# A two-layer streaming encoder: the four mixers run in 14 steps laid a projection apart, the row constants get a buffer of their own, and more of the conditioning is computed beside the mixers

## The chip, the cores and the metric

The kernel runs on one core of a Trainium2 chip. The metric is the device time of one execution in microseconds, from the first to the last instruction and what lies around them. Of three runs of the kernel before, the median was 1093.91 us (1090.06 to 1305.59). The rows below come from a further, profiled execution, which took 1088.88 us. The numbers are float32; a difference of about 2% is what a comparison of this kernel can tell from no change.

## The reference

One sequence of 256 tokens of width 1024 passes two layers. Each layer is a half-step SwiGLU FFN (width 2816), a token mixer, and a second half-step FFN; each is fed by an RMSNorm whose shift, scale and gate come from a vector c.

```python
for l in range(DEPTH):
    cond = (c_act @ ada_w[l] + ada_b[l])[:, None, :]
    sh1, sc1, g1, sh2, sc2, g2, sh3, sc3, g3 = jnp.split(cond, N_MOD, axis=-1)
    h = modulate(rmsnorm(x, norm_g[l, 0]), sh1, sc1)
    x = x + 0.5 * g1 * swiglu(h, ffn1_w13[l], ffn1_w2[l])
    h = modulate(rmsnorm(x, norm_g[l, 1]), sh2, sc2)
    x = x + g2 * hybrid_mixer(h, ...)
    h = modulate(rmsnorm(x, norm_g[l, 2]), sh3, sc3)
    x = x + 0.5 * g3 * swiglu(h, ffn2_w13[l], ffn2_w2[l])
return rmsnorm(x, final_g)
```

The mixer projects h to 3600 columns and splits them into four parts of width 256: forgetting attention (fox), mLSTM, retention with rotary (ret) and Mamba-2 SSD (ssd). Each makes a decayed score matrix per head, multiplies it with its values, and gates the result; the four results go through one output projection.

## The kernel before

Activations are kept feature-major (128 features by 256 tokens, eight tiles). Each float32 product is three matmuls on rounded parts: a weight tile `raw` of 128x1024 is loaded by a DMA on SP's queue, ScalarE (ACT) rounds it into `whi` (L199), VectorE (DVE) subtracts to get the rest `wlo` (L200), and TensorE (PE) adds `whi` by the high part of the input, `whi` by the low part and `wlo` by the high part (`mm3`, L215 to L219). So every 512 KB of weights cost DVE one *split* and PE 24 matmuls of about 256 columns. Four raw buffers and four pairs of split buffers let the loads and splits run ahead.

The conditioning matrix is 144 blocks of 128x1024. All but a few of the very first section are summed on DVE: a DMA loads a block into `araw`, and one DVE instruction (L258, here a *background sum*) multiplies it by c and adds up. The table `BG` says after how many projection or weight steps of a stage how many such blocks are put in; `flush` puts in what is missing before a stage needs it.

A stage starts with a normalisation: the sums of squares are reduced by two matmuls (`stat`, L346), ACT and POOL take the inverse root (`rs`, L367, L368), two matmuls spread it (L373) and ACT copies it to the row `R` (L377). The first two projections of a stage run on the unnormalised x (`uh`, `ul`), and their results are multiplied by R afterwards. All later ones need the normalised input: for each of eight tiles DVE makes `xr` (L402), ACT the high part `hh` (L406), DVE the low part `hl` (L407).

The mixers (`mixers_in`) are a list, `ORDER`: `p.rq` is the projection for `rq`, other names are steps that take a projection's result and run one part of a mixer. 14 projections of two weight tiles each run in the order of the list. `rotary` turns rq and rk (a 512-column matmul, then four DVE instructions), `gates` is a chain of some 20 small DVE instructions, `conv_silu` a convolution on DVE (L607), `ssd_front`, `ret_front`, `mlstm_front`, `fox_front` make score matrices (tiles `pp`, in PSUM banks `pb`), and `pv_tm` (L722) multiplies them with the values. In this list each mixer's scores and its product with the values are one step.

The order of instructions on an engine is set by a list scheduler in the framework: it keeps to the program's priorities (the order of the code, unless `tc.high_priority` raises a part) and to its own estimate of when inputs are ready. On the chip each engine runs its list strictly in order, and so does SP's DMA queue.

`row` (L628) holds 792 constants, sent to all 128 partitions by one DMA (L629) as the mixers begin; its tile takes memory that the FFN before it used. ACT reads it first in L821.

Of the kernel before, what the change touches and what calls it, by code (L numbers as in the profile page):

```python
# [15 lines left out]
P = 128  # L16
D = 1024
T = 256
# [22 lines left out]
WO_GROUPS = ((0, 1), (3, 2))  # L41

WO_TURNS = 2, 5
# [6 lines left out]
BG = [((16, 15), (5, 13), (6, 12)), ((8, 0), (5, 8)), ((14, 14), (6, 0), (10, 18)), ((14, 14), (6, 0), (10, 18)),  # L50
      ((8, 0), (5, 8)), ((14, 8),)]
R0 = 6
NW = 11, 0, 2, 6
HP, HP2 = 30, 100
ORDER = """p.rq p.rk rq h p.mv gates rk p.sx mv sx p.sbc sbc p.rv p.mq p.mk rows rv ssd p.fk mk mq mlstm p.fq
 ret fq p.fv fk fv p.sz sz fox p.mo foxb mo p.rg ssdb rg""".split()
# [5 lines left out]
def trunk_kernel(  # L62
# [119 lines left out]

    cond = [cp.tile([P, 72], F32, name=f"cond{l}") for l in range(L)]
# [137 lines left out]
    def stat_begin():  # L321
        s = Stat()
        s.R = s.rows = None
        s.ps = ps_c.tile([P, 2], F32, tag="c", name="stat")
        s.acc = tp.tile([P, T], F32, tag="acc", name="acc")
        s.sq = {}
        return s
# [43 lines left out]
    def stat_R(v, o, pin=False):  # L371
        for t in range(2):
            m = pe.matmul(o[:, t * P:(t + 1) * P], lhsT=v[:, t:t + 1].to_broadcast([P, P]), rhs=ident, start=True, stop=True)  # L373
            if pin:
                tc.keep_in_program_order(m)
        R = tp.tile([P, T], F32, tag="R", name="R")
        act.activation(out=R, in_=o[:, :T], func=AF.Copy)  # L377
        return R
# [138 lines left out]
    def ffn_in(fp, l, i, w13, w2, st, done):  # L517
# [47 lines left out]
        for c in range(NS if first else ND, NFF):  # L565
            if first and c == NS + 3:
                load_more()
            w = wload(w13(l, c), 2, KT, P)
            o = bank_a().rearrange("p (a b) -> p a b", a=2)
            mm_fm(o[:, 1, :], w[0], h)  # L570
            mm_fm(o[:, 0, :], w[1], h)
            gate_out(c, o[:, 0, :], o[:, 1, :])
            background()
# [42 lines left out]
    def mixers(l, st, done):  # L616
        with tc.tile_pool(name=f"mp{l}", bufs=1) as mp:
            bg_pool[:] = mp, 1
            spare[:] = None, 0
            return mixers_in(mp, l, st, done)  # L620

    def mixers_in(mp, l, st, done):
# [5 lines left out]
        row = mp.tile([P, NC_ROW], F32, name="row")  # L628
        sp.dma_start(out=row, in_=row_in[l].partition_broadcast(P))  # L629
# [222 lines left out]
        def ssd_front(sx, sc, la, dt):  # L852
# [54 lines left out]
        def ssd_back(xd, z2):  # L907
# [11 lines left out]
            turns.append((3, y))  # L919

        def mlstm_front(mlf, arow, mq, mv):
# [41 lines left out]
            num = pv_tm(*transpose_p(p0, p1), mv)  # L963
            return num, head_norm(num, "m", den)

        def fox_front(arow, fq):
# [23 lines left out]
            return p0, p1, den  # L990

        def fox_back(p0, p1, den, fv):
            num = pv_tm(*transpose_p(p0, p1), fv)
# [3 lines left out]
            put_y(0, to_fm(y))  # L997
# [12 lines left out]
        def ret_front(rq, rv):  # L1010
# [11 lines left out]
            dve.tensor_tensor(out=p1, in0=o.rearrange("p (h t) -> p h t", h=4), in1=dec[:, :, :P], op=ALU.mult)  # L1022
            num = pv_tm(p0, p1, rv)
# [24 lines left out]

        def e_rq():
            v["rq"] = mp.tile([P, 2, T], F32, tag="q", name="rq", bufs=2)  # L1050
            rotary(rotated("rq"), lambda r, rs: dve.tensor_tensor(out=v["rq"], in0=r, in1=rs, op=ALU.add))
# [27 lines left out]
        def e_ssd():  # L1079
            v["xd"] = ssd_front(v["sx"], v["sc"], v["la"], v["dt"])  # L1080
# [14 lines left out]
        def e_ret():  # L1095
            scaled(*ret_front(v["rq"], v["rv"]), "rl")

        def e_mlstm():
            scaled(*mlstm_front(v["gl"][:, :, 4:8], v["arow"], v["mq"], v["mv"]), "ml")
# [8 lines left out]
        def e_fox():  # L1108
            v["fp"] = fox_front(v["arow"], v["fq"])

        def e_foxb():
            fox_back(*v["fp"], v["fv"])
# [7 lines left out]
        def e_mo():  # L1120
# [8 lines left out]
            put_y(1, to_fm(y))  # L1129

        def e_rg():
# [4 lines left out]
            turns.append((2, y))  # L1136

        parts = dict(rq=e_rq, rk=e_rk, sx=e_sx, sbc=e_sbc, mv=lambda: e_v("mv"), rv=lambda: e_v("rv"), fv=lambda: e_v("fv"),
                     gates=e_gates, rows=e_rows, ssd=e_ssd, mq=e_mq, mk=e_mk, ret=e_ret, mlstm=e_mlstm, fq=e_fq, fk=e_fk,
                     fox=e_fox, foxb=e_foxb, sz=e_sz, ssdb=e_ssdb, mo=e_mo, rg=e_rg, h=lambda: h.extend(norm_h(st)))  # L1140
        for x in ORDER:
            if x.startswith("p."):
                project(x[2:])
            else:
                parts[x]()
# [6 lines left out]
        for g, grp in enumerate(WO_GROUPS):  # L1152
            for n, k in enumerate(WO_TILES):
# [172 lines left out]
```

## Time and profile before

| | |
|---|---|
| profiled execution | 1088.88 us, span 1087.1 us |
| runs, median (lowest to highest) | 1093.91 us (1090.06 to 1305.59) |
| PE busy | 1065.9 us, 98% of the span |
| PE weight loads busy | 1049.6 us, 97% |
| DVE busy | 853.6 us, 79% |
| ACT busy | 536.7 us, 49% |
| POOL busy | 69.8 us, 6% |
| granted TensorE clock | full speed in every slice |

The page gives, for the slowest (here the only) core, the busy time of each engine over the span, the costliest groups of instructions with the idle time just before them, and who ended that idle time. "A <- B: x" means that A sat idle for x us until B's result came. Two consecutive matmuls overlap in the records, so a record of 0.28 us starts 0.12 us after the one before it. The stages lie, in us from the span's start: FFN 0 to 199, mixers of layer 0 from 199 (their first normalisation ends at 220) to 350, FFN to 549, FFN of layer 1 to 727, mixers of layer 1 to 880, FFN to the end.

### The profile page before, as it was taken

The numbers are of one execution on the slowest core, as the hardware profiler recorded it, in microseconds if no ns is written. First come the engines' busy times: TensorE is split into PE (matmuls) and PEld (weight loads), VectorE is DVE, ScalarE is ACT, GpSimd is POOL, SyncE is SP. The second block draws the span as 40 slices with busy tenths as digits, with TensorE's granted clock in tenths as the row PEclk, the third lists the DMA queues.
The fourth block names the chain that finished last, engine by engine and source line by source line (L and its number), as shares of the span: only waits on it lengthen the run. The fifth ranks groups of instructions, "written<-read, shape, count | busy, mean of one in ns | idle before, by whom it ended". The sixth has DMA issues, their size and how long they took to land.

```text
span 1087.1 us, 21715 instructions
## 1 busy us (share of the span) xinstructions
PE 1065.9 (98%) x8745; PEld 1049.6 (97%) x8745; DVE 853.6 (79%) x1495; ACT 536.7 (49%) x893; POOL 69.8 (6%) x86
## 2 busy tenths in 40 slices
PE   8999999989999999999999999999999999999998
PEld 6999999989999999999999999999999999999998
DVE  6899889789957989888589888767987688876551
ACT  4555444355545745443474543355535566454441
POOL 0000001200012200000100000012001130000010
PEclk9999999999999999999999999999999999999999
DMA  9889989947424589888568988765644465865531
GB/s 367 333 299 347 324 323 329 304 160 244 143 97 154 187 293 343 296 294 284 187 213 280 333 302 303 265 203 192 222 147 142 131 214 195 290 225 183 184 126 40
DMA packets 73879, 258.17 MB, mean 237 GB/s; under 512 B 10161, under 2 KB 12465, under 8 KB 73266
## 3 DMA queue, kind: packets, MB, share of 16 engines
q1 hardware_dynamic: 73490, 256.26, 68.5%
q8 instruction: 69, 1.13, 0.4%
q10 hardware_dynamic: 288, 0.52, 0.1%
q14 instruction: 32, 0.26, 0.1%
HBM read 255.70 MB, written 1.05 MB: 236 GB/s over the span
## 4 chain that ended last, share of the span: by engine, by line
PE 78%; DMA 8%; DVE 8%; ACT 3%; issue 2%; POOL 1%; SPq 0%; ACTq 0%; DVEq 0%; POOLq 0%
PE pa L217 22%; PE pa L219 22%; PE pa L218 22%; DMA raw<-in_w2a_dram 3%; DMA araw<-in_ada_dram 3%; DVE wlo L200 2%; PE pa L678 2%; PE pa L676 2%; PE pa L677 1%; ACT whi L199 1%; DVE araw L258 1%; PE pb L729 1%; DVE ul L395 1%; ACT pp L987 1%; DMA row<-in_row_dram 1%
## 5 line engine op out<-in xcount | busy, mean ns | idle before, releaser
L199 ACT ACTIVATE whi<-raw 128x1024 fp32r<-128x1024 f32 (+1 forms) x340 | 354.1, 1046 | 287.7 <-PE pa L218 81.1
L200 DVE TENSOR_TENSOR wlo<-raw,whi 128x1024 fp32r<-128x1024 f32 (+1 forms) x340 | 409.1, 1211 | 87.8 <-ACT whi L199 87.1
L217 PE MATMUL pa<-hh,whi 128*128 128x256 f32 x1424 | 403.8, 284 | 1.5 <-ACT whi L199 0.8
L218 PE MATMUL pa<-hl,whi 128*128 128x256 f32 x1424 | 404.1, 284 | 0.0
L219 PE MATMUL pa<-hh,wlo 128*128 128x256 f32 x1424 | 403.0, 283 | 0.5 <-DVE wlo L200 0.5
L217 PEld LDWEIGHTS pa<-hh,whi 128*128 128x128 f32 x1424 | 273.2, 192 | 3.4 <-ACT whi L199 2.1
L219 PEld LDWEIGHTS pa<-hh,wlo 128*128 128x128 f32 x1424 | 273.2, 192 | 1.2 <-DVE wlo L200 0.7
L218 PEld LDWEIGHTS pa<-hl,whi 128*128 128x128 f32 x1424 | 273.3, 192 | 0.5 <-issue 0.5
L217 PE MATMUL pa<-sh,whi 128*128 128x256 f32 x704 | 199.2, 283 | 0.0
L218 PE MATMUL pa<-sl,whi 128*128 128x256 f32 x704 | 199.2, 283 | 0.0
L219 PE MATMUL pa<-sh,wlo 128*128 128x256 f32 x704 | 199.2, 283 | 0.0
L258 DVE CUSTOM_DVE_ANT_0 araw<-araw,cact 128x1024 f32<-128x1024 f32 x128 | 157.4, 1230 | 44.7 <-DMA araw<-in_ada_dram 44.2
L217 PEld LDWEIGHTS pa<-sh,whi 128*128 128x128 f32 x704 | 135.2, 192 | 0.0
L218 PEld LDWEIGHTS pa<-sl,whi 128*128 128x128 f32 x704 | 135.2, 192 | 0.0
L219 PEld LDWEIGHTS pa<-sh,wlo 128*128 128x128 f32 x704 | 135.2, 192 | 0.0
L534 ACT ACTIVATE sh<-s 128x256 fp32r<-128x256 f32 x88 | 36.1, 411 | 109.8 <-DVE s L527 104.7
L338 POOL TENSOR_TENSOR acc<-acc,sq 128x256 f32<-128x256 f32 x40 | 36.2, 906 | 697.8 <-ACT sq L333 696.8
L218 PE MATMUL pa<-ul,whi 128*128 128x258 f32 x208 | 59.1, 284 | 2.3 <-DVE ul L395 2.3
L217 PE MATMUL pa<-uh,whi 128*128 128x258 f32 x208 | 59.7, 287 | 0.0
L676 PE MATMUL pa<-whi,hh 128*128 128x256 f32 (+1 forms) x192 | 56.4, 294 | 3.1 <-ACT hh L406 3.1
L219 PE MATMUL pa<-uh,wlo 128*128 128x258 f32 x208 | 58.8, 283 | 0.0
L678 PE MATMUL pa<-whi,hl 128*128 128x256 f32 (+1 forms) x192 | 55.4, 292 | 0.0
(262 smaller groups left out, 1313.8 us busy)
## 6 DMA issues: line engine op xcount, KB each, us to landing
araw<-in_ada_dram SPq DMA_DIRECT2D x128, 512.0 KB, 5.6
raw<-in_w13b_dram SPq DMA_DIRECT2D x88, 512.0 KB, 5.0
raw<-in_w13a_dram SPq DMA_DIRECT2D x76, 512.0 KB, 5.9
raw<-in_w2a_dram SPq DMA_DIRECT2D x44, 512.0 KB, 5.5
raw<-in_w2b_dram SPq DMA_DIRECT2D x44, 512.0 KB, 4.6
raw<-in_wfm_dram SPq DMA_DIRECT2D x32, 512.0 KB, 4.9
raw<-in_wtm_dram SPq DMA_DIRECT2D x24, 512.0 KB, 4.4
raw<-in_wo_dram SPq DMA_DIRECT2D x16, 512.0 KB, 4.8
```

What stands on the lines that cost most here:

```text
L199: act.activation(out=hi, in_=raw, func=AF.Copy)
L200: dve.tensor_tensor(out=lo, in0=raw, in1=hi.bitcast(F32), op=ALU.subtract)
L217: pe.matmul(o, lhsT=wh, rhs=xh, start=first, stop=False, **kw)
L218: pe.matmul(o, lhsT=wh, rhs=xl, start=False, stop=False, **kw)
L219: pe.matmul(o, lhsT=wl, rhs=xh, start=False, stop=last, **kw)
L258: dve.tensor_tensor_reduce(out=raw, in0=raw, in1=cact, scale=0.5, scalar=0.0, op0=ALU.mult, op1=ALU.add, accum_out=cond[l][:, i:i + 1])
L338: eng.tensor_tensor(out=s.acc, in0=s.acc, in1=sq, op=ALU.add)
L395: dve.scalar_tensor_tensor(out=s.ul[:, k, :T], in0=xT[:, k, :], scalar=s.G[:, k:k + 1], in1=s.uh[:, k, :T].bitcast(F32), op0=ALU.mult, op1 ...
L534: act.activation(out=sh[:, c, :], in_=s, func=AF.Copy)
L676: pe.matmul(os[t], lhsT=h[0][:, k, ts], rhs=wh[:, y, :], start=(k == 0), stop=False)
L677: pe.matmul(os[t], lhsT=h[0][:, k, ts], rhs=wl[:, y, :], start=False, stop=False)
L678: pe.matmul(os[t], lhsT=h[1][:, k, ts], rhs=wh[:, y, :], start=False, stop=(k == KT - 1))
```

## The change

Five edits, of one piece each:

1. `ORDER` is rewritten. ssd, ret, mlstm and fox become generators that stop (`yield`) after their scores and, for mlstm and fox, before and after the transposes; each stop is one entry of the list, with at least one projection between. `rqe` takes rq's raw result out of PSUM, and `rq` (the rotary part) follows a projection later. ret runs before mlstm and within ssd; the gates sz and rg come before fox.
2. `row` becomes a buffer of its own (`rows_of`), loaded in the first FFN of each layer (`i == 0 and c == NS + 4`). To make room, `acc` and `R` have one buffer instead of two.
3. The normalisation `h` of the mixers is put at raised priority.
4. `BG` changes: 12 instead of 8 background sums are planned in the mixers of layer 0 and 14 instead of 8 in those of layer 1, spread over nearly all projections, with two `araw` buffers (`MB = 2`) instead of one; fewer in the second FFNs.
5. The output projection takes ssd and ret first, then fox and mlstm; the last fox step and two transposes lie between its first tiles (`WO_STEPS`).

The number of instructions of each kind is the same on every engine (8489 on PE, 1497 on DVE, 877 on ACT); only their order and buffers differ.

```diff
-WO_GROUPS = ((0, 1), (3, 2))
-WO_TURNS = 2, 5
+WO_GROUPS = ((3, 2), (0, 1))
-BG = [((16, 15), (5, 13), (6, 12)), ((8, 0), (5, 8)), ((14, 14), (6, 0), (10, 18)), ((14, 14), (6, 0), (10, 18)),
-      ((8, 0), (5, 8)), ((14, 8),)]
+BG = [((16, 17), (9, 21)), ((2, 0), (12, 12)), ((15, 16), (5, 0), (8, 12)), ((15, 16), (5, 0), (8, 12)),
+      ((14, 14),), ((14, 8),)]
+MB = 2
-ORDER = """p.rq p.rk rq h p.mv gates rk p.sx mv sx p.sbc sbc p.rv p.mq p.mk rows rv ssd p.fk mk mq mlstm p.fq
- ret fq p.fv fk fv p.sz sz fox p.mo foxb mo p.rg ssdb rg""".split()
+ORDER = """p.rq p.rk rqe h p.mv rq gates rk p.sx mv sx p.sbc sbc p.rv rows rv p.mq ssd ret p.mk ssd mq ret
+ p.sz ssd mk mlstm p.rg sz mlstm ssdb p.fk rg mlstm p.fq fk mlstm p.fv fq fox p.mo fv fox mo""".split()
+WO_STEPS = {1: "fox", 4: "turn", 6: "turn"}
...
-        s.acc = tp.tile([P, T], F32, tag="acc", name="acc")
+        s.acc = tp.tile([P, T], F32, tag="acc", name="acc", bufs=1)
...
+            if i == 0 and c == NS + 4:
+                rows_of[l] = cp.tile([P, NC_ROW], F32, tag="row", name="row", bufs=1)
+                sp.dma_start(out=rows_of[l], in_=row_in[l].partition_broadcast(P))
...
-        row = mp.tile([P, NC_ROW], F32, name="row")
-        sp.dma_start(out=row, in_=row_in[l].partition_broadcast(P))
+        row = rows_of[l]
...
             for t in range(2):
                 dve.tensor_tensor(out=xd[:, t], in0=ox.rearrange("p (t h d) -> p t h d", t=2, h=4)[:, t],
                                   in1=rw(R_D, 4).unsqueeze(2).to_broadcast([P, 4, 64]), op=ALU.mult)
+            yield
             num = pv_tm(e0, e1, v)
...
-            num = pv_tm(*transpose_p(p0, p1), mv)
+            yield
+            pt = transpose_p(p0, p1)
+            yield
+            num = pv_tm(*pt, mv)
...
+        def e_rqe():
+            v["rqe"] = rotated("rq")
...
+        def e_h():
+            with tc.high_priority(HP):
+                h.extend(norm_h(st))
...
+        def step(x):
+
+            if x not in running:
+                running[x] = parts[x]()
+            if running[x] is not None:
+                next(running[x], None)
...
-                if g == 0 and n in WO_TURNS:
-                    m, y = turns.pop(0)
-                    put_y(m, to_fm(y))
+                if g == 0 and n in WO_STEPS:
+                    step(WO_STEPS[n])
```

How the instructions move, at the three places of which the prediction speaks. First DVE in layer 0, after R is there (`xr`, `hl`: the normalised input's parts; `rsin`, `rraw`, `rq`: the rotary part). Before:

```order
L200 TENSOR_TENSOR wlo_2983<-raw_2980,whi_2982 128x1024
L407 SCALAR_TENSOR_TENSOR hl_2837<-xr_2838,cond0_89,hh_2836 128x256
L407 SCALAR_TENSOR_TENSOR hl_2837<-xr_2842,cond0_89,hh_2836 128x256
L1006 TENSOR_TENSOR rsin_2832<-pb_2830,tab_77 128x512
L1007 TENSOR_TENSOR rraw_2822<-rraw_2822,tab_77 128x512
L407 SCALAR_TENSOR_TENSOR hl_2837<-xr_2846,cond0_89,hh_2836 128x256
L1051 TENSOR_TENSOR rq_2821<-rraw_2822,rsin_2832 128x512
L407 SCALAR_TENSOR_TENSOR hl_2837<-xr_2850,cond0_89,hh_2836 128x256
```

and with the change:

```order
L405 SCALAR_TENSOR_TENSOR xr_2836<-xT_76,cond0_89,R_2770 128x256
L662 TENSOR_TENSOR rraw_2814<-pa_2692,R_2770 128x256
L410 SCALAR_TENSOR_TENSOR hl_2823<-xr_2824,cond0_89,hh_2822 128x256
L410 SCALAR_TENSOR_TENSOR hl_2823<-xr_2828,cond0_89,hh_2822 128x256
L410 SCALAR_TENSOR_TENSOR hl_2823<-xr_2832,cond0_89,hh_2822 128x256
L410 SCALAR_TENSOR_TENSOR hl_2823<-xr_2836,cond0_89,hh_2822 128x256
L405 SCALAR_TENSOR_TENSOR xr_2840<-xT_76,cond0_89,R_2770 128x256
L405 SCALAR_TENSOR_TENSOR xr_2844<-xT_76,cond0_89,R_2770 128x256
```

The rotary part and a split stood between the parts of h; now only one multiply of rq's raw result does.

Second, DVE in layer 1 in the middle of the mixers (`pp` with `dec`: ret's scores by their decay; `araw`: a background sum; `wlo_9876`: the second split of the projection mk). Before, these three products stood among mlstm's last steps:

```order
L1018 TENSOR_TENSOR pp_10229<-pb_10230,dec_9231 128x512
L835 TENSOR_REDUCE hv_10153<-hsq_10151 128x8
L1018 TENSOR_TENSOR pp_10229<-pb_10234,dec_9231 128x512
L837 TENSOR_TENSOR hv_10153<-hv_10153,den_10095 128x8
L1022 TENSOR_TENSOR pp_10229<-pb_10238,dec_9231 128x512
```

and with the change they stand right ahead of that split:

```order
L870 TENSOR_SCALAR st01_9843<-tab_77,lal_9829 128x128
L1029 TENSOR_TENSOR pp_9852<-pb_9853,dec_9212 128x512
L1029 TENSOR_TENSOR pp_9852<-pb_9857,dec_9212 128x512
L1033 TENSOR_TENSOR pp_9852<-pb_9861,dec_9212 128x512
L203 TENSOR_TENSOR wlo_9876<-raw_9873,whi_9875 128x1024
L261 ISA araw_9879,cond1_90<-araw_9879,cact_87 128x1024
```

So ret's scores moved forward, from the last third of the mixers to a place where a split is next in line behind them.

Third, SP's queue at the start of layer 0's mixers, before:

```order
L211 DMA raw_2980<-in_wfm_dram 128x1024
L211 DMA raw_2986<-in_wfm_dram 128x1024
L629 DMA row_2681<-in_row_dram 128x792
L631 DMA dec_2683<-in_dec_dram 128x1024
L255 DMA araw_3427<-in_ada_dram 128x1024
L211 DMA raw_3057<-in_wfm_dram 128x1024
```

and the row's load with the change, in the first FFN (`w13a` are its weights):

```order
L258 DMA araw_1017<-in_ada_dram 128x1024
L573 DMA row_1020<-in_row_dram 128x792
L214 DMA raw_1022<-in_w13a_dram 128x1024
```

The row's load left the mixers' start and lies in the first FFN, ahead of all its readers.

## Rows read from the trace of the kernel before

**Rows 1.** The page, busy us (share of the span) and instructions of each engine.

```profile
PE 1065.9 (98%) x8745; PEld 1049.6 (97%) x8745; DVE 853.6 (79%) x1495; ACT 536.7 (49%) x893; POOL 69.8 (6%) x86
```

**Rows 2.** Windows: start:end, us, then busy us of PE, PEld, DVE, ACT, POOL.

```profile
225.00:363.00 138.00, 133.06 (x1061) 128.88 (x1060) 114.57 (x258) 74.13 (x138) 15.80 (x17) 1.00 0.50 161
363.00:549.00 186.00, 185.78 (x1548) 185.56 (x1547) 152.37 (x239) 89.13 (x141) 6.16 (x7) 1.00 0.79 270
```

**Rows 3.** Waits of PE in layer 0's mixers: us in total, times, longest.

```profile
PE pb L373 <- POOL rs L368: 1.9, 1, 1.9
PE pa L676 <- ACT hh L406: 1.5, 1, 1.5
PE pa L218 <- DVE ul L395: 1.1, 2, 0.6
PE pb L729 <- DVE sv L897: 1.0, 1, 1.0
PE pb L879 <- DVE st L865: 0.7, 1, 0.7
PE pb L729 <- ACT pt L787: 0.5, 1, 0.5
```

**Rows 4.** Waits of PE in layer 1's mixers, beside two equal to rows 3.

```profile
...
PE pb L879 <- DVE st L865: 0.8, 1, 0.8
PE pb L729 <- DVE sv L897: 0.6, 1, 0.6
...
```

**Rows 5.** Timeline of ACT: start us, us, instruction, [idle before <- releaser].

```profile
218.58 0.20 ACT L821 ACTIVATE gea<-row 128x4 f32<-128x4 f32 x1 [6.17 <-DMA row<-in_row_dram]
218.69 0.24 ACT L367 ACTIVATE rs<-stat,epsc 128x2 f32<-128x2 f32 x1
220.94 0.39 ACT L377 ACTIVATE R<-pb 128x256 f32<-128x256 f32 x1
```

**Rows 6.** The chain that ended last, in order of time: start us, us, what.

```profile
219.78 0.71 PE pb L373 x4
276.46 1.33 PE pb L729 x10
748.21 0.44 PE pb L373 x4
```

**Rows 7.** Timeline of DVE around R in both layers.

```profile
219.97 2.49 DVE L200 TENSOR_TENSOR wlo<-raw,whi 128x1088 fp32r<-128x1088 f32 x2 [7.35 <-ACT whi L199]
222.38 0.75 DVE L657 TENSOR_TENSOR rraw<-pa,R 128x256 f32<-128x256 f32 x2
223.04 1.66 DVE L402 SCALAR_TENSOR_TENSOR xr<-xT,cond,R 128x256 f32<-128x256 f32 x4
750.64 0.75 DVE L657 TENSOR_TENSOR rraw<-pa,R 128x256 f32<-128x256 f32 x2
```

**Rows 8.** Waits of DVE for the background blocks: 221 to 300, then 749 to 829.

```profile
DVE araw L258 <- DMA araw<-in_ada_dram: 1.9, 2, 1.4
DVE araw L258 <- DMA araw<-in_ada_dram: 1.7, 2, 1.1
```

**Rows 9.** Timeline of DVE in layer 0, splits and a background sum.

```profile
262.41 2.36 DVE L200 TENSOR_TENSOR wlo<-raw,whi 128x1024 fp32r<-128x1024 f32 x2
264.69 1.22 DVE L258 CUSTOM_DVE_ANT_0 araw<-araw,cact 128x1024 f32<-128x1024 f32 x1
```

**Rows 10.** Windows of layer 0's mixers, columns as in rows 2.

```profile
223.00:271.00 48.00, 45.73 (x354) 43.63 (x353) 46.67 (x106) 26.05 (x44) 1.76 (x5) 1.00 0.62 205
```

**Rows 11.** The page's DMA issues: KB each, median us from issue to landing.

```profile
araw<-in_ada_dram SPq DMA_DIRECT2D x128, 512.0 KB, 5.6
```

**Rows 12.** Timeline of PE, rotary's matmul in layer 0.

```profile
225.36 1.02 PE L1002 MATMUL pb<-rraw,tab 128*128 128x512 f32 x2
```

More of the change, by code (lines that the diff above doesn't have):

```diff
@@ L181, in load_more @@
         dve.tensor_tensor(out=selR, in0=ident[:, :8], in1=ident[:, 32:40], op=ALU.add)
+    rows_of = {}
     cond = [cp.tile([P, 72], F32, name=f"cond{l}") for l in range(L)]
@@ L375, in stat_R @@
                 tc.keep_in_program_order(m)
-        R = tp.tile([P, T], F32, tag="R", name="R")
+        R = tp.tile([P, T], F32, tag="R", name="R", bufs=1)
         act.activation(out=R, in_=o[:, :T], func=AF.Copy)
@@ L617, in mixers @@
         with tc.tile_pool(name=f"mp{l}", bufs=1) as mp:
-            bg_pool[:] = mp, 1
+            bg_pool[:] = mp, MB
             spare[:] = None, 0
@@ L918, in ssd_back @@
                                          op0=ALU.mult, op1=ALU.mult)
-            turns.append((3, y))
+            put_y(3, to_fm(y))
         def mlstm_front(mlf, arow, mq, mv):
@@ L962, in mlstm_front, with fox @@
             dve.reciprocal(out=den, in_=den)
-            num = pv_tm(*transpose_p(p0, p1), mv)
+            yield
+            pt = transpose_p(p0, p1)
+            yield
+            num = pv_tm(*pt, mv)
             return num, head_norm(num, "m", den)
-        def fox_front(arow, fq):
+        def fox(arow, fq):
             p0, p1 = p_tiles()
@@ L989, in fox_front @@
             dve.reciprocal(out=den, in_=den)
-            return p0, p1, den
-        def fox_back(p0, p1, den, fv):
-            num = pv_tm(*transpose_p(p0, p1), fv)
+            yield
+            pt = transpose_p(p0, p1)
+            yield
+            num = pv_tm(*pt, v["fv"])
             y = mp.tile([P, 2, 256], F32, tag="y", name="fy", bufs=2)
@@ L996, in fox_back @@
                               in1=den.unsqueeze(2).to_broadcast([P, 8, 64]), op=ALU.mult)
-            put_y(0, to_fm(y))
+            turns.insert(0, (0, y))
         def rotary(o, outs):
@@ L1022, in ret_front @@
             dve.tensor_tensor(out=p1, in0=o.rearrange("p (h t) -> p h t", h=4), in1=dec[:, :, :P], op=ALU.mult)
+            yield
             num = pv_tm(p0, p1, rv)
@@ L1047, in rotated @@
             return r
+        def e_rqe():
+            v["rqe"] = rotated("rq")
         def e_rq():
             v["rq"] = mp.tile([P, 2, T], F32, tag="q", name="rq", bufs=2)
-            rotary(rotated("rq"), lambda r, rs: dve.tensor_tensor(out=v["rq"], in0=r, in1=rs, op=ALU.add))
+            rotary(v["rqe"], lambda r, rs: dve.tensor_tensor(out=v["rq"], in0=r, in1=rs, op=ALU.add))
         def e_rk():
@@ L1079, in e_ssd @@
         def e_ssd():
-            v["xd"] = ssd_front(v["sx"], v["sc"], v["la"], v["dt"])
+            v["xd"] = yield from ssd_front(v["sx"], v["sc"], v["la"], v["dt"])
         def e_mq():
@@ L1095, in e_ret @@
         def e_ret():
-            scaled(*ret_front(v["rq"], v["rv"]), "rl")
+            scaled(*(yield from ret_front(v["rq"], v["rv"])), "rl")
         def e_mlstm():
-            scaled(*mlstm_front(v["gl"][:, :, 4:8], v["arow"], v["mq"], v["mv"]), "ml")
+            scaled(*(yield from mlstm_front(v["gl"][:, :, 4:8], v["arow"], v["mq"], v["mv"])), "ml")
         def e_fq():
@@ L1108, in e_fox @@
         def e_fox():
-            v["fp"] = fox_front(v["arow"], v["fq"])
-        def e_foxb():
-            fox_back(*v["fp"], v["fv"])
+            return fox(v["arow"], v["fq"])
         def e_sz():
@@ L1128, in e_mo @@
                                      op0=ALU.mult, op1=ALU.mult)
-            put_y(1, to_fm(y))
+            turns.append((1, y))
         def e_rg():
@@ L1135, in e_rg, with e_turn @@
                                      op0=ALU.mult, op1=ALU.mult)
-            turns.append((2, y))
-        parts = dict(rq=e_rq, rk=e_rk, sx=e_sx, sbc=e_sbc, mv=lambda: e_v("mv"), rv=lambda: e_v("rv"), fv=lambda: e_v("fv"),
-                     gates=e_gates, rows=e_rows, ssd=e_ssd, mq=e_mq, mk=e_mk, ret=e_ret, mlstm=e_mlstm, fq=e_fq, fk=e_fk,
-                     fox=e_fox, foxb=e_foxb, sz=e_sz, ssdb=e_ssdb, mo=e_mo, rg=e_rg, h=lambda: h.extend(norm_h(st)))
+            put_y(2, to_fm(y))
+        def e_h():
+            with tc.high_priority(HP):
+                h.extend(norm_h(st))
+        parts = dict(rqe=e_rqe, rq=e_rq, rk=e_rk, sx=e_sx, sbc=e_sbc, mv=lambda: e_v("mv"), rv=lambda: e_v("rv"), fv=lambda: e_v("fv"),
+                     gates=e_gates, rows=e_rows, ssd=e_ssd, mq=e_mq, mk=e_mk, ret=e_ret, mlstm=e_mlstm, fq=e_fq, fk=e_fk,
+                     fox=e_fox, sz=e_sz, ssdb=e_ssdb, mo=e_mo, rg=e_rg, h=e_h)
+        running = {}
+        def step(x):
[3 more added lines that the diff above has]
+                next(running[x], None)
+        def e_turn():
+            for m, y in turns:
+                put_y(m, to_fm(y))
+                yield
+        parts["turn"] = e_turn
         for x in ORDER:
@@ L1144, in mixers_in @@
             else:
-                parts[x]()
+                step(x)
         flush(l, 5)
```

## The prediction, made blind

> **What bounds the kernel.** I read the page first: PE is busy 1065.9 us and all else less [rows 1]. The reader is to see that this leaves 21.2 us of the 1087.1 us span in which PE does nothing, and that no edit here takes an instruction off PE, so the change can at most take waits out. Then the windows by stage: an FFN keeps PE busy 185.78 of 186 us, the mixers of layer 0 133.06 of 138 [rows 2]. So nothing can be won in the FFNs, and what moves there counts only if it makes PE late. Then who PE waits for in the mixers. In layer 0: 1.9 us for the inverse root, 1.5 for the normalised input, 0.7 and 1.0 for two of ssd's tables, 0.5 for a transposed score, together 5.6, and 1.1 for `ul` at the end [rows 3]. In layer 1 there is none for the root: 1.5 and 0.5 in the same words as the rows for `hh` and `pt` in [rows 3], and 0.8 and 0.6 [rows 4], together 3.4. The 9.0 us of both layers are the stake. DVE, which most of these waits name, is busy 46.67 of 48 us in the first third of the mixers [rows 10]: it has no room there, and what is late on it makes PE late.
>
> **A balance for DVE.** How late DVE is at a tile for PE is its start after the statistics, plus the work in its list up to that tile, plus its own waits, minus PE's work up to there. Before, at ssd's product with the values in layer 0: the two matmuls that spread the root start at 219.78, the product at 276.46 [rows 6], 56.7 us apart, of which PE waited 1.5 + 0.7 + 1.0 = 3.2; so PE had 53.5 of work. DVE's first work with R starts at 222.38 [rows 7], 2.6 after the statistics. Its list up to the ssd values counts 16 normalising instructions of 0.41 (1.66 for four [rows 7]), 14 splits and 5 background sums of 1.14 (two splits from 262.41, the next start at 264.69 [rows 9]), 16 convolution steps of about 0.41 and 64 others, about 51.7 in all. Of its waits 1.9 were for background blocks [rows 8]. 2.6 + 51.7 + 1.9 - 53.5 = 2.7, near the 3.2 waited. So the balance works to about half a microsecond, and I use it for the new order.
>
> **The change, part by part.**
>
> *Row constants.* In layer 0 ACT stood 6.17 us for the row's DMA, and only then, at 218.69, computed the root [rows 5]; PE's 1.9 us follow from that [rows 3]. With the load in the first FFN this goes: -1.9. The bounds are 0 (something else holds ACT) and -1.9; in layer 1 PE has no such wait [rows 4], so I take -1.9. It also frees the two splits of the next weights, for which DVE stood 7.35 us [rows 7] and which then ran after R was due. Without that, R is ready 0.71 us after the matmuls start plus a copy of 0.39 [rows 5, 6], so DVE starts about 1.2 after the statistics instead of 2.6, and in layer 1 instead of 750.64 - 748.21 = 2.4 [rows 6, 7]. The row's load beside the FFN's weights and the single buffers of `acc` and `R` I cost at 0: PE has 0.22 us idle in a whole FFN [rows 2], the next use of either buffer is a stage away; if the cover went, a block's landing is 5.6 us [rows 11], which is the bound above.
>
> *The normalised input first.* Up to the last low part DVE now has 16 x 0.41 + one multiply of 0.38 = 7.0, with the start 8.2. PE needs it after the rest of rk (the rotary matmul behind it starts at 225.36 [rows 12], 5.6 after 219.78) and 21 matmuls of the next projection at 0.13, 8.3. They meet; I leave 0.5 of the 1.5 in layer 0.
>
> *Layer 0, the steps.* Up to ssd's product the new list has 12 splits, 6 sums, 15 convolution steps and ret's three products of 0.6: again 51.7. PE has more ahead of it: ret's scores and ret's own product (about 2.6 each; ten records of such a product span 1.33 [rows 6] and it has 24) and 8 more projection matmuls (1.0), so 59.7. DVE is there 1.2 + 51.7 + 0 to 1.9 - 59.7, 5 to 7 us early. Both ssd waits go, and the transposed scores of mlstm and fox have a projection in between. The tightest place is the second split of rv: list 23.5, start 1.2, PE 24.7, so level; I leave 0.5. Layer 0 then waits 1.0 instead of 5.6.
>
> *Layer 1, the steps and the sums.* Here sums are planned from the first projection on. At the second split of mk, right behind ret's three products, the list counts 16 normalising instructions (6.5), 11 splits (12.5), 5 sums (5.8), 12 convolution steps (4.9) and 16.0 of others, 45.7; PE has 308 projection matmuls of 0.12 (185.78 us for 1548 [rows 2]), ret's scores, the row sums and the rotary, about 43.3. 1.2 + 45.7 + 0.5 of own waits - 43.3 = 4.1 late. This takes the place of the 3.4 that go. From below it could be 1.5 (no own waits, sums that find room in FFN time before R), from above 7, if DVE waits for blocks as it did (1.7 [rows 8]) and starts as late as now.
>
> *The rest.* Fewer sums in the second FFNs give nothing, since PE is full there. The tail (the output projection, `ul`) has the same DVE list; 1.1 stays.
>
> *Sum.* 5.6 + 3.4 go, 1.0 + 4.1 come: -3.9 on 1088.88, so 1085.0 for a profiled execution. Bounds: -9.0 (nothing comes) and about +1. The runs shown lie above the profiled one, the nearest by 1.2 and the median by 5.0; I take the 1.2 and predict **1086**.
>
> [...] In layer 0's window the weight loads are busy 128.88 of 138 us, PE 133.06 [rows 2]. [...]
>
> **The rivals.**
> - *All covers hold* (23%). The sums in layer 1 find DVE early, because it starts 1.2 us sooner and no longer waits 1.7 for blocks. For it: two block buffers. Against it: the 45.7 against 43.3. All 9.0 go: about 1081.
> - *It does not do what it says* (10%). The waits only change names in both layers, because a chain of DVE, PE and ACT was what took the time and DVE stays full for the first third; only the 1.9 for the root goes, or not even that: 1087 to 1094, about 1090.
> - *Slower by background blocks* (14%). With two buffers a block's load can start only when the sum before last is done, and lands 5.6 us later [rows 11]. Two sums closer than (5.6 + 1.14) / 2 = 3.4 us apart on average leave DVE waiting for a block, with splits behind it. Up to the turn of ssd's result the lists have 8 and 9 sums. If each waits 1.4, as the longest one did [rows 8], that is 23.8, less the 3.6 there were and some 6 that layer 0 has in hand: 14 more, 1100. Against it: one sum per projection is 5.9 us apart, wider than 3.4.
> - *Weight loads as the measure* (3%). If the further 4.2 us a layer between PE's and the loads' idle time were waits that the steps fill, 8.4 more would go than in the first rival: about 1073. [...]
>
> **The numbers.** My forecast has 50%, its own range 1082 to 1091. The range 1079 to 1096 leaves out the last rival, most of the third and a little of the first, 16% together. 2%, about what a measurement of this kernel can tell, is 21.9 us: faster by that needs more than all 21.2 us of PE's idle time, or the last rival and luck (2%); slower by that needs the third rival at nearly twice its price (3%); within it 95%.
>
> **What would show it.** Right: no wait of PE for the root in layer 0, DVE's first work with R within 1.5 us of the spread; ssd's two waits gone in both layers; in layer 1 a wait of PE for `wlo` of 2 to 5 us in the first 45 us after R. Wrong: PE waits for `wlo` in layer 0 of over 2 us (my balance has the wrong work or start), DVE idle for blocks of over 2 us a layer (the slower rival), or any new idle time in the FFNs (loads late behind the moved row or sums).

## The result: 0.7% slower where 0.4% faster was forecast

The changed kernel takes 1102.92 us in the median of 11 runs (1100.33 to 1105.63), the kernel before 1094.84; the ratio is 1.007, with an interval of 1.0048 to 1.0093. One of the eleven runs of the kernel before took 1305.59 us and is not in the ratio. The forecast was 1086, by a sum that took off 3.9 us, with a range of 1079 to 1096: the sign was wrong and the time lies outside. The loss, like every ratio below, is smaller than the 2% that a comparison of this kernel can tell; its interval leaves out 1, and where an interval below does not, the text says so. The page after, engines and granted clock in 40 slices:

```profile
PE 1071.2 (97%) x8745; PEld 1053.3 (96%) x8745; DVE 855.1 (78%) x1495; ACT 537.4 (49%) x893; POOL 71.8 (7%) x86
PEclk9999999999999999999999999998999999999999
```

PE, DVE and ACT have as many instructions as in [rows 1], 8745, 1495 and 893 (the other counts given with the change stand in no page), but the span is 1102.7 us, and one slice, at 744 to 772 us, shows a lower clock. PE's idle time grew from 21.2 to 31.5 us, and its busy time by 5.3 us with the same instructions. I divide the span at the first matmul of `stat` of each normalisation; the four around the mixers are, after (PE's timeline: start us, us, instruction, [idle before]):

```profile
219.80 0.86 PE L349 MATMUL stat<-tab,acc 128*128 128x1 f32 x4 [2.82 <-POOL acc L341]
370.86 0.50 PE L349 MATMUL stat<-tab,acc 128*128 128x1 f32 x4
...
754.31 0.50 PE L349 MATMUL stat<-tab,acc 128*128 128x1 f32 x4
905.53 0.50 PE L349 MATMUL stat<-tab,acc 128*128 128x1 f32 x4
```

A mixers stage is the difference of two such rows: 151.1 in layer 0 and 151.2 in layer 1. Windows between the same rows (columns as in [rows 2]) give the first FFN of layer 0 and the two mixers stages, before:

```profile
9.68:215.12 205.44, 204.11 (x1716) 200.16 (x1717) 180.42 (x294) 100.12 (x152) 11.30 (x14) 1.00 0.91 330
215.12:362.07 146.95, 140.12 (x1118) 135.73 (x1117) 118.67 (x265) 78.34 (x148) 16.51 (x18) 1.00 0.51 165
745.44:890.02 144.58, 139.89 (x1117) 135.65 (x1116) 118.63 (x265) 78.46 (x148) 16.52 (x18) 1.00 0.51 169
```

and after:

```profile
9.56:219.80 210.24, 204.90 (x1716) 200.22 (x1717) 179.44 (x289) 99.85 (x153) 10.12 (x12) 1.00 0.89 318
219.80:370.86 151.06, 142.89 (x1115) 137.48 (x1116) 123.12 (x274) 78.98 (x148) 19.52 (x21) 0.99 0.54 179
754.31:905.53 151.22, 142.34 (x1117) 137.89 (x1116) 125.12 (x278) 78.36 (x147) 16.69 (x18) 0.98 0.54 179
```

In the FFN PE's idle time went from 1.3 to 5.3 us; in the mixers it went from 6.8 to 8.2 and from 4.7 to 8.9, and PE was busy 2.8 and 2.5 us longer at a lower mean clock. The same stages in the profiles that the argument rests on, in us:

| kernel | median us | first FFN of layer 0 | mixers 0 | mixers 1 |
|---|---|---|---|---|
| before | 1094.84 | 205.4 | 147.0 | 144.6 |
| changed | 1102.92 | 210.2 | 151.1 | 151.2 |
| e1, old sums, one buffer | 1086.30 | 205.3 | 144.1 | 144.5 |
| e10, old sums, two buffers | 1081.72 | 207.5 | 141.5 | 141.4 |
| e13, e10 with two sums at the head of mixers 1 | 1089.97 | 206.8 | 141.5 | 149.8 |
| e14, e10 with the new row of the first FFN | 1090.77 | 208.3 | 148.4 | 141.5 |

The first FFN is counted from its own `stat`, at 9 to 11 us; the other FFNs agree within 0.7 us in all of these. The profiled execution of the change is 15.6 us above that of before (4.8 + 4.1 + 6.6, and 0.1 elsewhere); the medians are 8.1 apart, because before's profiled execution is near the lowest of its runs (e12) and the changed kernel's is 1.6 above its median.

**Where PE waits now.** Layer 0 from 199 us, then layer 1 from 740:

```profile
PE stat L349 <- POOL acc L341: 2.8, 1, 2.8
PE pa L681 <- DVE cva L613: 2.4, 1, 2.4
PE pa L681 <- DVE rraw L662: 2.3, 1, 2.3
PE pa L222 <- DVE wlo L203: 1.3, 3, 0.7
...
PE pa L681 <- DVE rraw L662: 5.3, 1, 5.3
PE pa L222 <- DVE wlo L203: 0.7, 2, 0.4
```

The root's 1.9 and the waits for `st`, `sv` and `pt` of [rows 3, 4] are gone, as forecast. The 2.8 stand at the end of the FFN, ahead of layer 0's statistics. In the mixers PE now waits at the first matmul of the third projection, mv, for `rraw`. That is not an operand: rq and rk fill all four `pa` banks, and mv gets its bank only when DVE has multiplied rq's first result out of it. The 2.4 for `cva` are of the same kind, later in the list: a bank that the convolution on DVE still reads.

**Why `rraw` is late.** DVE's timeline in layer 1; the spread of R by PE is at 756.92, its copy on ACT at 758.08:

```profile
757.87 1.22 DVE L261 CUSTOM_DVE_ANT_0 araw<-araw,cact 128x1024 f32<-128x1024 f32 x1 [4.57 <-DMA araw<-in_ada_dram]
759.02 0.08 DVE L261 DVE_READ_ACCUMULATOR2_ANT cond<- 128x1 f32 x1
759.02 1.28 DVE L203 TENSOR_TENSOR wlo<-raw,whi 128x1088 fp32r<-128x1088 f32 x1
760.22 1.22 DVE L261 CUSTOM_DVE_ANT_0 araw<-araw,cact 128x1024 f32<-128x1024 f32 x1
...
761.37 1.67 DVE L405 SCALAR_TENSOR_TENSOR xr<-xT,cond,R 128x256 f32<-128x256 f32 x4
...
767.31 0.75 DVE L662 TENSOR_TENSOR rraw<-pa,R 128x256 f32<-128x256 f32 x2
```

DVE stands 4.57 us in front of a background sum whose block is still on its way (it was issued at 750.56 and took 7.3 us to land), with mv's split behind it, then takes a second sum. Its first work with R starts at 761.37, 3 us after R is there, and `rraw` stands behind 15 instructions of the normalised input. Before, `rraw` was the first work with R [rows 7]. Layer 0 has one such sum, behind a longer wait; `rraw` comes fifth there:

```profile
226.25 1.23 DVE L261 CUSTOM_DVE_ANT_0 araw<-araw,cact 128x1024 f32<-128x1024 f32 x1 [7.15 <-DMA araw<-in_ada_dram]
...
229.81 1.67 DVE L405 SCALAR_TENSOR_TENSOR xr<-xT,cond,R 128x256 f32<-128x256 f32 x4
231.39 0.42 DVE L662 TENSOR_TENSOR rraw<-pa,R 128x256 f32<-128x256 f32 x1
```

**The clock.** Windows around layer 1's wait (columns as in [rows 2]; the figure before the DMA share is the granted clock):

```profile
754.00:762.00 8.00, 8.00 (x69) 8.00 (x69) 4.13 (x7) 3.95 (x8) 1.01 (x2) 1.00 0.77 295
762.00:766.00 4.00, 0.59 (x6) 0.39 (x4) 4.00 (x11) 3.54 (x9) 0.00 (x0) 1.00 0.74 248
766.00:774.00 8.00, 6.13 (x31) 6.16 (x32) 8.00 (x15) 3.20 (x8) 0.00 (x0) 0.57 0.37 112
774.00:780.00 6.00, 6.00 (x41) 5.04 (x40) 5.04 (x12) 2.21 (x4) 0.50 (x3) 1.00 0.87 308
```

In the 8 us from 766 on, of which the first 1.9 belong to the wait, the clock is 0.57, and in each single us from 767 to 772 it is 0.50; PE was busy for 6.13 of the 8, so by an estimate from these two figures (1 - 0.57) x 6.13 = 2.6 us were lost beside the 5.3. Layer 0 has the same behind the 2.8 us in front of its statistics:

```profile
220.00:224.00 4.00, 4.00 (x22) 4.00 (x22) 0.00 (x0) 1.58 (x5) 1.74 (x4) 0.57 0.96 354
```

That is another 1.7 us by the same estimate, and it falls into the mixers stage though the wait lies in the FFN. The two make 4.3 of the 5.3 us that PE is busy longer.

### The profile page after: what moved, and what is told of

It reads as the page before. It is cut to its first block, busy times and chain, and to the rows that moved or that the text cites. A ratio compares the mean times of both kernels' runs of the same rounds, so it can differ in the third digit from the quotient of the medians.

```text
span 1102.7 us, 21703 instructions
## 1 busy us (share of the span) xinstructions
PE 1071.2 (97%) x8745; PEld 1053.3 (96%) x8745; DVE 855.1 (78%) x1495; ACT 537.4 (49%) x893; POOL 71.8 (7%) x86
```

## The experiments

Theory A was that sums at the head of the mixers, and the normalised input ahead of the evictions, make DVE late. Rival B was that the steps cost the time. Four kernels cross the two.

**e1.** `BG` as before and `MB = 1`; all else as changed.

```diff
-BG = [((16, 17), (9, 21)), ((2, 0), (12, 12)), ((15, 16), (5, 0), (8, 12)), ...
+BG = [((16, 15), (5, 13), (6, 12)), ((8, 0), (5, 8)), ((14, 14), (6, 0), (10, 18)), ...
-MB = 2
+MB = 1
```

> The changed kernel with the sums' table and the single block buffer of the kernel before; steps, early row and high priority of the normalised input stay. Theory A (two faults at the head of the mixers: a background sum stands ahead of the normalised input on DVE, and the four evictions of rq and rk behind it): the 4.8 us lost before layer 0's statistics go, and the sums ahead of the first normalising instruction (4.6 us late in layer 0, 3.0 in layer 1), but PE still waits some 2 us a layer for the evictions: profiled time 1093 to 1097, 7 to 11 below the changed kernel. Rival B (the steps a projection apart cost the time, whatever the sums): within 3 us of the changed kernel, 1100 to 1105.

Measured: 1086.30 (1085.69 to 1087.69), ratio to before 0.9916 (0.9884 to 0.9947). Rival B falls; the table cost more than theory A said, and no wait for `rraw` is left, though the high priority is still there.

**e2.** `h` at plain priority, table as changed.

```diff
-            with tc.high_priority(HP):
-                h.extend(norm_h(st))
+            h.extend(norm_h(st))
```

> The changed kernel with the normalised input at plain priority, so that the first two evictions stand ahead of it on DVE again; sums as changed. Theory A: PE's waits for rraw (2.3 and 5.3 us) turn into waits for the normalised input of at most 2 us a layer, and the half-speed stretches behind them shrink; the 4.8 us ahead of layer 0's statistics and the sums at the head of DVE stay: 1096 to 1100, 4 to 8 below the changed kernel. Rival C (the evictions are not what PE waits for; with DVE late by the sums the wait only changes its name): 1102 to 1105, and PE's wait at the first matmul of the third projection keeps its length in layer 1.

Measured: 1104.63, ratio 1.0078 (1.0048 to 1.0109), as the change. The half of theory A on the evictions falls, and rival C has the time right. `rraw` is early again, and PE waits 4.0 us for `hh` in layer 0, and in layer 1 for mv's split, which stands behind the sums:

```profile
PE pa L682 <- DVE wlo L203: 3.4, 2, 2.5
```

**e3.** Both edits.

> Both edits of the two kernels before this: steps and early row of the change, with the sums' table, the single block buffer and the plain priority of the kernel before. Theory A: nothing of the loss is left, and the mixers' steps may bring a few us: 1084 to 1091. Rival B (the steps cost the time): 1096 or more.

Measured: 1087.20, ratio 0.9928 (0.9902 to 0.9955): as e1, so the priority is worth nothing with the old sums either.

**e4.** Old steps, early row, new table and two buffers.

> The kernel before with the early row in its own buffer, and the sums' table and two block buffers of the change; steps as before, normalised input at plain priority. Theory A: the 4.8 us ahead of layer 0's statistics come here too, and in layer 1 the sums ahead of the first normalising instruction make PE wait some 2 us more: 1092 to 1097 profiled, above the kernel before by 4 to 8. Rival B (the steps cost the time, not the sums): 1085 to 1089, no more than the kernel before.

Measured: 1103.75, ratio 1.0084 (1.0055 to 1.0114). The new table costs under the old steps too, more than expected: mixers of 156.5 and 149.4 us, with DVE 10.23 us in front of one block at the head of layer 0.

**e5 to e7: which rows of the table.** e5 has the first FFN's old row, e6 the mixers' old rows and one buffer.

> The changed kernel with the first FFN's row of the sums' table as in the kernel before (40 sums planned there, not 38); the mixers' rows, the two block buffers and everything else stay as changed. If the first FFN's plan is what makes the weights late at its end, the stage up to layer 0's statistics falls from 210.2 to about 205.4 us, and the mixers keep their 151.1 and 151.2: 1097 to 1100. If that stage is long for another reason (the early row in the queue), it stays near 210 and the time at 1102 to 1105.

Measured: 1096.10, ratio 1.0012 (0.999 to 1.0034); the interval holds 1. The stage ahead takes 207.2, and the mixers fell as well, to 148.5 and 149.0, which was not expected. For layer 0 e14 shows why. Layer 1 has the same rows as in the change; there DVE's wait at the head was 3.65 instead of 4.57 and PE's for `rraw` 4.4 instead of 5.3, so 2.2 us can lie between two executions with the same sums in this stage.

> The changed kernel with the mixers' rows of the sums' table and the single block buffer as in the kernel before; the FFNs' rows stay as changed. If the sums in the mixers cost, the two mixers stages fall from 151.1 and 151.2 us to about 144.1 and 144.5, but in layer 0 the first FFN's last sum still stands ahead of the normalised input and keeps up to 3 us of it, and the stage ahead stays near 210: 1090 to 1095. If the mixers are long for another reason than their sums: 1099 or more.

Measured: 1108.45, ratio 1.013 (1.0099 to 1.0161): a miss, and no clean test. The FFNs' new rows leave 14 sums for layer 1's mixers; with 8 planned, `flush` puts the other six in a row at their end, where PE waits 6.4 us for `uh`. The table's rows belong together. One thing it does show: with the mixers' old row and one buffer DVE still stands 7.43 us in front of a first sum at layer 0's head, as in the change.

e7 keeps 12 and 14 sums in the mixers, but all late:

```diff
-... ((2, 0), (12, 12)), ... ((14, 14),) ...
+... ((6, 0), (8, 12)), ... ((5, 0), (9, 14)) ...
```

> As the kernel with the first FFN's old row, and the mixers' 12 and 14 sums all planned behind the fifth or sixth projection, none in the first third; two block buffers. Theory P (the place costs: sums at the head of the mixers, where DVE has no room): both mixers stages come back to 144 to 146 us, 1085 to 1090. Rival N (the number costs: 4 and 6 more sums of 1.22 us on DVE and as many more block loads): the mixers stay 4 to 7 us a layer above 144, 1093 to 1099.

Measured: 1094.57, ratio 1.0001 (0.998 to 1.0023), which holds 1. Layer 0 comes back to 144.7, layer 1 stays at 150.6, though no sum stands at the head of either. Against e10 (141.5, 141.4) that is 3.1 and 9.2 us for 4 and 6 more sums: the head alone is not the whole of it. Either the number costs, or that so many stand close together in what is left of the list.

**e9: the old number at the new place.** 8 sums in each mixers stage, from the third and the first projection on.

> The changed kernel with the FFNs' rows of the sums' table as before, and in each mixers stage the old number, 8 sums, but at the change's place: from the third projection on in layer 0 and from the first in layer 1; two block buffers. Theory P (the place costs): PE waits 3 to 5 us for rraw in layer 1 as in the change, its mixers stage is 147 to 150 us, the time 1091 to 1096. Theory N (the number costs): both mixers stages 144 to 145, 1086 to 1088.

Measured: 1096.34, ratio 0.9991 (0.9966 to 1.0017), which holds 1; mixers 148.3 and 148.5, PE's wait for `rraw` 4.1 in layer 1. So the place alone costs some 7 us a layer against e10. And beside e5, which has 12 and 14 sums at the same places and takes 148.5 and 149.0, the number costs no more than half a microsecond there (the medians differ by 0.2; the rows for the two FFNs between the mixers differ as well). So what e7 shows is more likely that sums late in the list stand too close; no run tested that alone.

**e8, e11: what the change is good for without its table.** e8 is the kernel before with the early row and single `acc` and `R`; e11 is e1 with the row loaded at the mixers' start.

> The kernel before with the early row in its own buffer (and single buffers for the sum of squares and the spread root), nothing else. If the row is all that the change is good for, this gives what the change with the old sums gave, 1085 to 1088, in as narrow a range of runs. If the steps bring part of it: 1088 to 1092, with PE's waits for ssd's tables of 0.7 and 1.0 us still there.

Measured: 1092.26 (1086.75 to 1097.11), ratio 0.9974 (0.9946 to 1.0003): too little to tell from nothing by the runs. But the two profiled executions have the same mean clock, 1.000, and there the span is 1085.0 against 1087.1, layer 0's mixers take 145.0 against 147.0, and PE's wait for the root is gone, which agrees with the 1.9 us forecast for the row. PE's waits for the tables stay (`sv` 1.8 and `st` 1.4 over both layers).

> The kernel with the old sums of the first experiment, with the row constants loaded at the start of the mixers again, so that the steps are all that is left of the change. If the early row brings 1.9 us: 1088 to 1090, with PE waiting up to 2 us for the root in layer 0. If the steps bring it all: 1085 to 1088.

Measured: 1088.28, ratio 0.9935 (0.991 to 0.996). The steps bring most. Whether the median's 2.0 us to e1 are the row's is not shown: e11's row keeps a buffer of its own and is issued at 200.39 us, where before's was at 211.58, so ACT waits 1.0 for it and PE only 0.5 for the root in the whole kernel. Between 200 and 225 us of e11 PE waits for weights and for the sum of squares:

```profile
PE pa L219 <- ACT whi L201: 1.8, 1, 1.8
PE stat L348 <- POOL acc L340: 1.3, 1, 1.3
PE pa L221 <- DVE wlo L202: 0.8, 1, 0.8
```

**e10: two buffers under the old table.** e1 with `MB = 2`.

> The kernel with the old sums of the first experiment, with two block buffers in the mixers instead of one. If the second buffer costs (earlier block loads in front of weight loads on the queue): 1089 to 1093 and a stage up to layer 0's statistics of 207 us or more. If not: 1085 to 1088.

Measured: 1081.72 (1081.28 to 1082.09), ratio 0.9858 (0.981 to 0.9906): the fastest kernel, ahead of both. I expected a loss or nothing. DVE's waits for blocks inside the mixers fell from 3.0 and 4.6 us (e1) to 0.4 and none, and PE's whole list of waits in layer 1's mixers is:

```profile
PE pa L220 <- DVE ul L397: 1.2, 2, 0.6
PE pb L713 <- DVE sy L923: 0.6, 2, 0.3
PE pb L375 <- POOL rs L370: 0.3, 1, 0.3
```

Its DVE at the head of layer 1 has no sum, and `rraw` is the fifth work with R:

```profile
744.66 2.49 DVE L202 TENSOR_TENSOR wlo<-raw,whi 128x1088 fp32r<-128x1088 f32 x2 [3.81 <-ACT whi L201]
747.07 1.67 DVE L404 SCALAR_TENSOR_TENSOR xr<-xT,cond,R 128x256 f32<-128x256 f32 x4
748.66 0.42 DVE L661 TENSOR_TENSOR rraw<-pa,R 128x256 f32<-128x256 f32 x1
```

**e13, e14: one piece each, on e10.** e13 plans two of layer 1's 8 sums at its first two projections:

```diff
-... ((8, 0), (5, 8)), ((14, 8),)]
+... ((2, 2), (6, 0), (5, 6)), ((14, 8),)]
```

> The fastest kernel so far (steps, early row, two block buffers, old sums; its mixers stages 141.5 and 141.4 us) with two of layer 1's 8 mixers sums moved to its first two projections, nothing else. Theory H (a block load that lands late, at the head of DVE's list, is enough): PE waits 3 us or more for rraw in layer 1, its stage goes to 145 to 149, layer 0's stays at 141 to 142, the time 1085 to 1089. Rival (two sums cost what two sums take, 2.4 us of DVE at most, and mostly beside other work): layer 1 within 141 to 143, 1081 to 1083.

Measured: 1089.97, ratio 0.993 (0.9895 to 0.9965); layer 1's mixers take 149.8, 8.3 us more than in e10, and no other stage grew by more than 0.6. The other six sums came forward with the two (the last at 801.2 us, in e10 at 833.5), so the price is not of two sums alone; but of PE's waits only 0.7 for `g` and 0.6 for `cva` are new beside the one at the head. The same place of its DVE list:

```profile
745.54 1.23 DVE L260 CUSTOM_DVE_ANT_0 araw<-araw,cact 128x1024 f32<-128x1024 f32 x1 [4.72 <-DMA araw<-in_ada_dram]
...
747.90 1.22 DVE L260 CUSTOM_DVE_ANT_0 araw<-araw,cact 128x1024 f32<-128x1024 f32 x1
...
749.04 1.67 DVE L404 SCALAR_TENSOR_TENSOR xr<-xT,cond,R 128x256 f32<-128x256 f32 x4
...
754.98 0.75 DVE L661 TENSOR_TENSOR rraw<-pa,R 128x256 f32<-128x256 f32 x2
```

R's first work is 2.0 us later than in e10, and `rraw` 6.3: with sums in the list the scheduler also laid `rraw` behind the normalised input. PE waits 5.4 us there, and in 752 to 760 us the clock is 0.57. So theory H holds, with an order that makes it worse; stage and time lie 0.8 and 1.0 us above the ranges given for it.

> The fastest kernel so far with the first FFN's row of the sums' table as in the change (38 sums planned, and the two that are left over in layer 0's mixers, behind the eighth projection). If that row costs: the last sum of the FFN stands ahead of the normalised input, DVE waits for its block, and with the weights late at the FFN's end the two first stages come to 352 to 356 us together in place of 349.0: 1085 to 1090. If it doesn't: 1081 to 1083.

Measured: 1090.77, ratio 0.9942 (0.9905 to 0.9978); the two first stages 356.7 instead of 349.0. The mechanism is that of e13, but the sum is not the FFN's last: all 38 of that row are done ahead of it. With the new row, layer 0's mixers hold 10 sums instead of 8, and the scheduler hoists one of them, planned behind the eighth projection, to DVE's head:

```profile
224.37 1.23 DVE L260 CUSTOM_DVE_ANT_0 araw<-araw,cact 128x1024 f32<-128x1024 f32 x1 [7.25 <-DMA araw<-in_ada_dram]
```

Of the 6.9 us that this mixers stage is longer than e10's, 3.4 are busy time of PE: the clock is 0.60 in 220 to 224 us, behind a wait of 1.7 for the sum of squares, and 0.57 in 230 to 234, behind one of 2.3 for `rraw`.

**e12: before again.** Unchanged.

> The kernel before once more, unchanged, for a trace of an execution nearer to its median. Spans and clocks of its runs so far lie on a line of about 1.1 us for each 0.001 of the mean granted clock below 1. If the clock is what sets its runs apart: a span of 1088 plus 1.1 us per 0.001, and stretches at the lower clock right behind PE's waits in the mixers. Rival (late loads set them apart): new waits of PE for weights, at a clock of 0.998 or more.

Measured: 1090.98, span 1089.2 at a clock of 0.998; the line gives 1090.2. The same wait of PE for the root, in the kernel before's profiled execution and then in this one:

```profile
216.00:220.00 4.00, 2.11 (x18) 1.90 (x16) 0.03 (x1) 1.42 (x6) 0.71 (x1) 1.00 0.75 277
220.00:224.00 4.00, 4.00 (x35) 4.00 (x35) 4.00 (x7) 2.72 (x6) 0.00 (x0) 1.00 0.36 112
```

```profile
216.00:220.00 4.00, 1.93 (x17) 1.72 (x16) 0.00 (x0) 1.23 (x3) 0.71 (x1) 1.00 0.65 262
220.00:224.00 4.00, 4.00 (x22) 4.00 (x23) 3.85 (x6) 1.52 (x5) 0.00 (x0) 0.59 0.37 102
```

35 matmuls in 4 us at full clock, 22 at 0.59. The wait is the same within 0.2 us; whether the clock falls differs from run to run. Where it fell, layer 0's mixers took 149.3 us instead of 147.0. The spans of 25 runs of before, 1087.4 to 1101.2, rise by about 1.1 us for each 0.001 of the mean granted clock below 1 (correlation 0.87).

**e15: the wait filled.** The changed kernel, with 12 matmuls into a bank that nothing reads, where PE waits for `rraw`:

```diff
                 h.extend(norm_h(st))
+            o = bank_b()
+            for _ in range(12):
+                tc.keep_in_program_order(pe.matmul(o, lhsT=tabR[:, 0, :], rhs=tabR.rearrange("p a b -> p (a b)"),
+                                                   start=True, stop=True))
```

> The changed kernel with 12 matmuls of 512 columns added in each layer behind the second projection, right where PE waits for rraw, into a bank that nothing reads: some 2.8 us of work of no use in waits of 2.4 and 5.4 us. If the lower clock behind the waits is brought by the wait: no stretch at 0.5 to 0.6 behind it in layer 1, its stage 1 to 2 us shorter, and the time 1099 to 1103 though work was added. If the clock falls for another reason: the stretches stay, and the time is that of the change or up to 1 us more, 1102 to 1106.

Measured: 1103.17, ratio to before 1.0046 (1.0025 to 1.0067): its interval and that of the change overlap, and the time alone decides nothing. In layer 1 the clock did not fall in the profiled execution, though PE still waits 1.6 us behind the filling:

```profile
762.00:766.00 4.00, 3.41 (x18) 2.57 (x16) 4.00 (x11) 3.08 (x8) 0.00 (x0) 1.00 0.65 221
766.00:774.00 8.00, 7.02 (x51) 6.57 (x52) 7.70 (x15) 3.82 (x8) 0.45 (x1) 1.00 0.44 141
```

51 matmuls in the 8 us in place of 31, and layer 1's mixers 149.5 instead of 151.2 us with 2.9 us of work added (e5, with the same sums there and no filling, took 149.0, so the stage's length proves little). Layer 0's grew by 1.1, with a wait of 3.2 for `rraw` a few matmuls behind the filling; over the whole execution the mean clock is 0.998, where that of the change is 0.994. In the four executions with an unfilled wait for `rraw` at layer 1's head, of 5.3 (the change), 5.4 (e13), 4.4 (e5) and 4.1 us (e9), the clock was 0.57 over 4 to 8 us at or behind the wait's end. So in layer 1 the clock went with the wait, 1.00 with the filling and 0.57 without, as far as five executions show it. As a cure the filling is worth nothing here.

## Why the prediction was wrong, step by step

- *Row constants*: right in its first half. PE's 1.9 us for the root are gone, in e8 too. The second half, "DVE starts about 1.2 after the statistics", is the step that failed. By the marks that I set, DVE's first work with R should start within 1.5 us of the spread; it started 229.81 - 224.05 = 5.8 us after it in layer 0 and 761.37 - 756.92 = 4.5 in layer 1:

```profile
224.05 0.61 PE L376 MATMUL pb<-tab,rs 128*128 128x128 f32 x4
756.92 0.61 PE L376 MATMUL pb<-tab,rs 128*128 128x128 f32 x4
```

  I took the wait for the row away and did not ask what DVE's list held in that gap: splits before, and now a background sum ahead of them. The order of the change shows it; I read the list from the first work with R on and counted the sums without their places.
- *The normalised input first*: 0.5 us was left for it; 2.3 and 5.3 came. I compared DVE with PE at the operand, `hh` and `hl`, and not at the bank that `rraw` frees. e3 against e1 shows that the raised priority is not to blame; in layer 1 the scheduler puts `rraw` behind four of the normalising instructions without sums at the head and behind 15 of 16 with them (e10 against e13).
- *Layer 0, the steps*: right. e10 has none of the waits that I struck out, and a mixers stage of 141.5 where before has 147.0. In the change that gain lies under the table's loss, 9.5 us.
- *Layer 1, the steps and the sums*: forecast was a wait for the second split of mk, 4.1 us; for `wlo` PE waits 0.7 there. The balance counted the sums as work (1.2 us each). At DVE's head a sum cost the landing of its block too, for which DVE stood 4.57 us here and 4.72 in e13, and all that was queued behind it: with two of them there the stage took 8.3 us more (e13).
- *The rest*: the first FFN was costed at nothing, with the 0.22 us of idle time of an FFN as the reason; that row is layer 0's second FFN, with the DMA engines busy 0.79 of the time, where the first has 0.91. It is 4.8 us longer in the profile, and 4.0 of them are idle time of PE: 2.8 for the sum of squares at its end, the others for weights. e14, which has that row alone, waits 1.7 for the sum of squares and is idle 3.6 us there, against 1.7 in e10; it is only 0.8 longer, since e10's execution ran part of this stage at a lower clock (0.66 in 16 to 21 us).
- *The clock* was costed at nothing too: before's profiled execution had a mean clock of 1.000 (a 9, which is 0.90 or more, in every slice; 0.95 in the last 10 us), and the sum has no term for it. PE was busy 5.3 us longer, by the estimates above mostly behind the two waits.
- *The rival that came* is the slower one by background blocks, at 14%, with 1100 against 1102.92. Its mark, DVE idle for blocks of over 2 us a layer, is met: 8.2 and 7.2. Its mechanism, sums too close together for two buffers, is met only in small part, by one wait of 1.0 and one of 2.6 some 100 us into the stages: a long wait at the head, 7.15 and 4.57, makes the rest, and two buffers by themselves bring 4.6 us (e10 against e1). That its 1100 lies near the measured time is luck.
- *All covers hold*, 1081: that is e10, 1081.72, once the table is undone.
- *Weight loads as the measure*, 1073 at 3%: not reached. e10's page has the loads idle for 29.6 us of its span of 1080.3 and PE for 14.2:

```profile
PE 1066.1 (99%) x8745; PEld 1050.7 (97%) x8745; DVE 856.3 (79%) x1495; ACT 536.0 (50%) x893; POOL 66.9 (6%) x86
```

  The loads are idle 15.4 us longer than PE there; no run here showed work to fill that time.
- *The base*: I laid the forecast 1.2 us above the profiled execution. Its mean clock was 1.000, and most executions of before are not like that (e12). The runs of e1, which has fewer waits, lie closer together: six span 2.0 us.

So the change is three things: steps and early row, -0.84% (e1); a second buffer, with them -1.42% (e10); and a table of sums that brings it to +0.7%. That table's loss is 21.2 us in the medians. Put on e10 one at a time, sums at the head of layer 1's mixers cost 8.3 us (e13), the first FFN's row 9.1 (e14), and the new place in both mixers 14.6 (e9); taken out of the change, the first FFN's row gives back 6.8 (e5). These overlap, since e9 and e14 both put a sum at layer 0's head, and they do not add up to the whole; how they share it was not taken apart.

## What to carry to other kernels

Background work has a place, not only a price: look in each engine's list for what stands ahead of the first instruction that the bound engine waits for, and ask of each such piece whether its load can have landed. Where the bound engine waits, ask what frees its output bank as well as what makes its operands. And when a change holds several pieces, a loss of the whole says little about any of them: here two of three pieces were worth 1.4% together, and the table of numbers took back more than both gave.

## What the runs showed of the hardware

- A wait of TensorE cost more than its length here. At the end of a wait of 5.3 us and behind it the granted clock was 0.57 over 8 us, another 2.6 us by the estimate above; behind the 2 us for the root it stayed at 1.00 in one execution of before and was 0.59 for 4 us in another. In the one execution where the long wait was filled with useless matmuls, down to 1.6 us, it stayed at 1.00.
- A block of 512 KB lands 5.6 us after its issue in the page's median [rows 11]; at the head of layer 1's mixers one took 7.3 us, and in layer 0 such a block held DVE for 7.15 us, in e4 for 10.23.
